# A's first head group in natural token order with 2 or 3 key blocks per query block, and factors per token spread by way of DRAM

## The chip, the cores and the metric

The kernel runs on one core of one Trainium2 chip. The metric is the device time of one execution in microseconds (us), the median of several. Engines: PE (TensorE; PEld is its weight load), DVE (VectorE), ACT (ScalarE), POOL (GpSimd) and SP (SyncE). In this kernel SP's queue issues the weight loads and POOL's queue issues transfers of intermediate data.

## The reference, cut to what matters

An encoder of two layers on 512 tokens of width 1024. Each layer projects the normalised input by one wide matrix and feeds three branches. Only the parts that the change touches stand here:

```python
DEPTH, SEQ, D_MODEL = 2, 512, 1024
A_GROUPS = ((128, 1), (512, 4), (2048, 16))   # (window, dilation), two heads of 64 each
def layer(x):
    xn = rms_norm(x, norm1_g)                  # one factor per token
    aq, ak, av, bq, bk, bv, cq, ck, cv, cg, gates = split(xn @ w_in)
    # A: each query attends to i + dilation*j, |j| <= window/(2*dilation), softmax;
    #    group outputs are weighted by their shares of the softmax denominators
    o, lse = dilated_window_attention(rope(norm(aq)), rope(norm(ak)), av, dilation, half)
    ya = o * softmax(lse over groups)          # one factor per token and head
    yb = rms_norm(diff_attention(...), b_out_norm_g) * c             # 4 heads of 128
    yc = silu(cg) * rms_norm(bidirectional_retention(...), c_out_norm_g)   # 4 heads of 128
    g = sigmoid(gates)
    x = x + (g0 * (ya @ w_br_a) + g1 * (yb @ w_br_b) + g2 * (yc @ w_br_c)) @ w_o
    x = x + square(relu(rms_norm(x, norm2_g) @ w_mlp1)) @ w_mlp2
```

A's first group has window 128 and dilation 1: a query sees the 64 tokens before and after it, so in natural order a block of 128 queries meets keys of its own block and of the neighbours at either side only.

## The kernel before, in words

All tensors are fp32. Each operand of a large product is split in two fp32r parts (`xh`, `xl`; `hi`, `lo`), and three products stand for one (`mm3`, `gemm`). Weights come in units of 512 KB at most by SP's queue into four raw buffers; `refine` has ACT make `whi` and DVE make `wlo` of each, two units ahead of PE, in three buffers each. `gemm` accumulates a chunk in four PSUM banks (`acc0` to `acc3`), which DVE or ACT evacuate while PE goes on with the next chunk.

Activations between the large products have the feature in the partition and the 512 tokens along the row. Token 4p+j stands in column 128j+p, so each of the four blocks of 128 columns holds every fourth token. In that order the window of A's first group (heads with g = 0) reaches into all four blocks: `a_dense_scores` (L650) scores a block of 128 queries against all 512 keys and adds a mask, and `dense_out` (L562) turns all 16 blocks of 128x128 over by PE transposes (`to_keys`, L535, tile ps_to_keys), splits them and multiplies them by V (tile ps_a_tail). The groups with dilation 4 and 16 need only blocks on the diagonal (`a_diag_scores`, `a_diag_out`).

A factor per token (the RMS factors of the two norms, the norm factor of each B or C head, the shares of A's groups) is computed on DVE with the token in the partition, as a tile of 128x4 or 128x24. To scale a tile that has the feature in the partition, the factor must stand along the row in all partitions. `norm_spread` (L423) broadcasts the factor along the row and transposes it on PE (tile ps_norm), and ACT copies it out as `rB`. `thread_a` (L709) copies A's shares to 128x512 (`wx`) and transposes them (ps_thread_a). `head_norm` (L579) transposes the head's output y to tokens in partitions (ps_yt), takes sums of squares, scales there by the factor (`yn`), transposes back (ps_yb), and then applies gain and gate.

Order: `build` makes one program of all operations. The main thread is the chain of gemms in the order of `sequence`; the side threads (prep, A, B, C, norm of a head) yield after each piece, with a lag in PE time (`W`). `emit` (L1064) then puts the program into one queue per engine: at each step the operation that can start first by the kernel's own reckoned durations, and among several the one that stands first in the program. A transfer by POOL counts 1.0 there, and 2.0 until its data can be used. Each engine then runs its queue in that order; an operation whose input is late holds up all that stands behind it on its engine.

POOL's queue before holds only 24 transfers: in each layer the eight residual tiles `xr` loaded ahead of the output projection, and between the layers the eight stores of `xspill`.

Of the kernel before, what the change touches and what calls it, by code (L numbers as in the profile page):

```python
# [9 lines left out]
FT = mybir.dt.float32  # L10
# [6 lines left out]
P = 128  # L17
# [10 lines left out]
C_ID, C_DL, C_U, C_M1, C_M2 = 0, 128, 1024, 1920, 2048  # L28
C_CP, C_SP, C_CC, C_SC, C_END = 2176, 2208, 2240, 2496, 2752
# [13 lines left out]
def shape_constants():  # L43
# [5 lines left out]
    blob[:, C_U:C_M1] = np.where(np.abs(dl) <= 64, 0.0, NEG).reshape(P, 896)  # L49
# [63 lines left out]
class Trunk:  # L113
# [202 lines left out]
    def setup(self):  # L316
# [31 lines left out]
        self.xspill = [a["x"], self.dp.tile([KD, P, SEQ], FT, name="xspill")]  # L348

# [121 lines left out]
    def prep(self, w, jp):  # L471
# [38 lines left out]
        own = [slice(64 * m, 64 * m + 64) for m in range(2)]  # L510
        for m in range(2):
            self.act(qk[own[m], m:4:2, qs], b[own[m]])
# [9 lines left out]
    def score(self, w, ms, j, pss, n=None):  # L522
        qk = w["qk"]
        js = slice(j * P, (j + 1) * P)
        ks = slice(0, SEQ) if n is None else js
# [36 lines left out]
    def dense_out(self, vt, ws, av):  # L562
        for jk in range(NJ):
            hi, lo = self.to_keys(ws, jk)
            yield ("wait", "av")
            if isinstance(vt, tuple):
                self.av_all(av, vt, jk, hi, lo, jk == 0, jk == NJ - 1)
            else:
                self.mm(av, vt[:, jk, :], hi, jk == 0, False)
                self.mm(av, vt[:, jk, :], lo, False, jk == NJ - 1)  # L570
            yield
# [7 lines left out]
    def head_norm(self, l, branch, h, y, s):  # L579
# [8 lines left out]
        for j in range(NJ):  # L588
            self.act(y[:, j * P:(j + 1) * P], b[:, j * P:(j + 1) * P], AF.Square, accum_out=ss[:, j:j + 1])
# [6 lines left out]
        else:  # L596
# [3 lines left out]
        yn = self.U(name="yn")  # L600
        self.tt(yn.rearrange("p (j e) -> p j e", j=NJ), b.rearrange("p (j e) -> p j e", j=NJ),
                g[:, :, None].to_broadcast([P, NJ, P]), OP.mult)
        yield ("wait", "yb")
        b2 = self.ps(name="ps_yb")
        for j in range(NJ):
            self.tr(b2[:, j * P:(j + 1) * P], yn[:, j * P:(j + 1) * P], self.ident)
        out = self.y[l, branch]
        if branch == 1:
            out[h] = self.split(b2, "yn", scale=gain)
        else:  # L610
            self.stt(yn, b2, gain, self.silu[l][h], OP.mult, OP.mult)
            self.silu[l][h] = None
            yield
            out[h] = self.split(yn, "yn")
# [34 lines left out]

    def a_dense_scores(self, w, m, st, nmx, den):  # L650
        for j in range(NJ):
            ps = self.ps(name="ps_a_dense_scores")
            self.score(w, (m,), j, (ps,))
            sm = self.U(name="sm")
            mx = self.tiny(1, "mx1")
            mask = self.blob[:, C_U - P + (3 - j) * P:C_U - P + (7 - j) * P]
# [52 lines left out]
    def thread_a(self, l):  # L709
# [5 lines left out]
        for g in range(3):  # L715
# [3 lines left out]
            n_, d_ = nmx[:, g * 8:g * 8 + 8], den[:, g * 8:g * 8 + 8]  # L719
            for m in range(2):  # L720
# [6 lines left out]
                tail = self.a_tail(l, w, m, g, st, ys)  # L727
        yield from tail
        nm = self.tiny(8, "amin", 2)
# [3 lines left out]
        for g in range(3):  # L733
# [485 lines left out]
```

## Time and profile before

| | |
|---|---|
| median of 3 runs | 1721.14 us (1721.01 to 1721.66) |
| profiled execution | 1721.42 us, span 1719.6 us (1.8 us lie outside the span) |
| granted TensorE clock, mean | 1.000 |
| PE busy | 1709.5 us (99%) |
| DVE busy | 1094.3 us (64%) |
| ACT busy | 813.0 us (47%) |
| POOL busy | 13.3 us (1%) |
| DMA | 93 GB/s over the span |

Matmuls of PE overlap, so the time that one takes of the engine is the distance between starts, not its own duration. "Idle before" names what an engine waited for. The layers are alike; the first one's attention part lies between 30 and 450 us, its MLP follows until 860 us, and the second layer repeats this.

### The profile page before, as it was taken

The page shows a single profiled execution, that of the slowest core. Times are in us where ns is not written, and L with a number is a line of the kernel's source. Part 1 is how long each engine was busy: PE and PEld are TensorE (multiplying, and loading weights), DVE is VectorE, ACT ScalarE, POOL GpSimd, SP SyncE. Part 2 cuts the span into 40 slices and gives each one's busy share as a digit, 9 for nine tenths or more (in the row PEclk, how much of TensorE's full clock was granted, in tenths as well). Part 3 has the DMA queues.
Part 4 walks back from the last instruction along what each step waited for, and adds up shares of the span by engine and source line. Part 5 has one row for each costly group of instructions (what it writes and reads, how often), then busy time and mean ns, then how long its engine had stood idle before and what let it go on. Part 6 is the DMA issues. An engine that isn't in the chain of part 4 may idle for free. (4 is left out here: it accounts for less than half of the span.)

```text
span 1719.6 us, 21537 instructions
## 1 busy us (share of the span) xinstructions
PE 1709.5 (99%) x8120; PEld 1454.8 (85%) x8120; DVE 1094.3 (64%) x2126; ACT 813.0 (47%) x1529; POOL 13.3 (1%) x29
## 2 busy tenths in 40 slices
PE   8999999999999999999999999999999999999999
PEld 8889988888888888888898899888888888888887
DVE  8788897887655343434468788888867543434342
ACT  7676674655344232323457666646543441414141
POOL 0000000000000000000000000000000000000000
PEclk9999999999999999999999999999999999999999
DMA  6212212223322222222332222222232222222221
GB/s 222 106 60 72 83 56 95 78 74 105 104 98 98 98 98 98 98 95 93 107 123 86 71 68 78 80 74 86 74 123 90 96 97 98 98 98 98 98 92 68
DMA packets 47960, 160.64 MB, mean 93 GB/s; under 512 B 5616, under 2 KB 6256, under 8 KB 47728
## 3 DMA queue, kind: packets, MB, share of 16 engines
q1 hardware_dynamic: 45072, 151.84, 26.0%
q0 software_dynamic: 1920, 6.29, 1.0%
q8 instruction: 64, 1.05, 0.2%
q10 hardware_dynamic: 864, 1.13, 0.2%
q14 instruction: 40, 0.33, 0.1%
HBM read 155.05 MB, written 4.19 MB: 93 GB/s over the span
## 5 line engine op out<-in xcount | busy, mean ns | idle before, releaser
L185 DVE TENSOR_TENSOR wlo<-raw,whi 128x1024 fp32r<-128x1024 f32 (+2 forms) x297 | 345.0, 1162 | 456.7 <-ACT whi L175 456.0
L175 ACT ACTIVATE whi<-raw 128x1024 fp32r<-128x1024 f32 (+2 forms) x297 | 300.2, 1011 | 629.8 <-PE acc L224 560.7
L224 PE MATMUL acc<-xgh,whi 128*128 128x512 f32 x960 | 377.1, 393 | 0.0
L224 PE MATMUL acc<-xgl,whi 128*128 128x512 f32 x960 | 374.7, 390 | 0.0
L224 PE MATMUL acc<-xgh,wlo 128*128 128x512 f32 x960 | 374.2, 390 | 0.0
L224 PEld LDWEIGHTS acc<-xgh,wlo 128*128 128x128 f32 x960 | 180.3, 188 | 37.6
L224 PEld LDWEIGHTS acc<-xgh,whi 128*128 128x128 f32 x960 | 180.3, 188 | 37.4 <-DVE gate L194 0.8
L224 PEld LDWEIGHTS acc<-xgl,whi 128*128 128x128 f32 x960 | 180.4, 188 | 36.1
L224 PE MATMUL acc<-whi,xgh 128*128 128x384 f32 (+1 forms) x576 | 202.5, 355 | 6.0 <-ACT whi L175 5.5
L224 PE MATMUL acc<-wlo,xgh 128*128 128x384 f32 (+1 forms) x576 | 201.7, 350 | 0.0
L224 PE MATMUL acc<-whi,xgl 128*128 128x384 f32 (+1 forms) x576 | 201.3, 349 | 0.0
L224 PE MATMUL acc<-hh,whi 128*128 128x512 f32 x512 | 199.2, 389 | 0.0
L224 PE MATMUL acc<-hl,whi 128*128 128x512 f32 x512 | 199.2, 389 | 0.0
L224 PE MATMUL acc<-hh,wlo 128*128 128x512 f32 x512 | 199.2, 389 | 0.0
L224 PEld LDWEIGHTS acc<-whi,xgh 128*128 128x128 f32 x576 | 108.8, 189 | 13.0 <-ACT whi L175 5.8
L224 PEld LDWEIGHTS acc<-wlo,xgh 128*128 128x128 f32 x576 | 109.2, 189 | 6.0 <-DVE wlo L185 0.3
L224 PEld LDWEIGHTS acc<-whi,xgl 128*128 128x128 f32 x576 | 109.0, 189 | 5.3
L224 PEld LDWEIGHTS acc<-hl,whi 128*128 128x128 f32 x512 | 96.1, 188 | 20.0
L224 PEld LDWEIGHTS acc<-hh,wlo 128*128 128x128 f32 x512 | 96.1, 188 | 19.9
L224 PEld LDWEIGHTS acc<-hh,whi 128*128 128x128 f32 x512 | 96.1, 188 | 19.9
L175 ACT ACTIVATE qk<-ps_prep 64x512 fp32r<-64x512 f32 (+1 forms) x144 | 69.8, 485 | 20.3 <-DVE qk L185 11.4
L185 DVE TENSOR_TENSOR xr<-xr,acc 128x512 f32<-128x512 f32 (+1 forms) x81 | 54.6, 678 | 30.6 <-PE acc L224 30.1
(199 smaller groups left out, 2225.3 us busy)
## 6 DMA issues: line engine op xcount, KB each, us to landing
raw<-in_weights_dram SPq DMA_DIRECT2D x236, 512.0 KB, 3.2
raw<-in_weights_dram SPq DMA_DIRECT2D x55, 384.0 KB, 3.0
xt<-in_x_dram SPq DMA_DIRECT2D x8, 256.0 KB, 5.1
xr<-in_x_dram POOLq DMA_DIRECT2D x8, 256.0 KB, 3.9
xspill<-xr POOLq DMA_DIRECT2D x8, 256.0 KB, 2.5
xr<-xspill POOLq DMA_DIRECT2D x8, 256.0 KB, 3.5
blob<-in_blob_dram SPq DMA_DIRECT2D x1, 1024.0 KB, 8.4
raw<-in_weights_dram SPq DMA_DIRECT2D x4, 256.0 KB, 2.6
```

The lines of the kernel that those rows point to most:

```text
L175: lambda: self.nc.scalar.activation(out, in_, func, **k))
L185: self.dve(out, [out], [a, b], lambda: self.nc.vector.tensor_tensor(out, a, b, op=op))
L224: self.op("PE", d, [out], [lhsT, rhs], lambda: self.nc.tensor.matmul(out, lhsT, rhs, start=start, stop=stop))
```

## The change

Three edits.

1. A's first group keeps queries, keys and values in natural token order. `keep_in_order` writes queries and keys into natural order while they are evacuated from PSUM; `reorder` stores V (two tiles of 256 KB) to DRAM and loads it back in four pieces each; a block of queries is scored against the 2 or 3 blocks next to it, with a mask table of three blocks; `band_out` transposes 10 blocks in three groups (4, 3 and 3) where 16 were transposed, and multiplies with 256 or 384 columns. The output goes back to the old token order as it is evacuated, and the statistics (8 minima, 8 denominators per partition) go back by way of DRAM (`reorder_stats`).
2. `norm_spread` becomes `spread`: the tile of factors is stored to DRAM as rows of 512, and a load that reads the same row for all partitions puts it along the row. The same serves A's shares (6 rows, 64 partitions each) and the norm factor of each B and C head, which is then applied to y itself, in the feature layout, so the transpose back goes.
3. The sum of squares writes its unused product to PSUM, so that y stays.

```diff
     def norm_spread(self, r):
-        b2 = self.ps(name="ps_norm")
-        for j in range(NJ):
-            self.tr(b2[:, j * P:(j + 1) * P], r[:, j:j + 1].to_broadcast([P, P]), self.ident)
-        rB = self.U(name="rB")
-        self.act(rB, b2)
-        return rB
+        return self.spread(r, 1, "rB")[0]
+
+    def spread(self, r, n, name, rows=P):
+
+        d = self.dp.tile([n, SEQ], FT, name=self.uid("row"))
+        self.dma(self.nc.gpsimd, d.rearrange("i (j p) -> p (i j)", j=NJ), r, 2)
+        out = []
+        for i in range(0, n, P // rows):
+            t = self.U(name=name)
+            for h in range(P // rows):
+                v = d[i + h]
+                self.dma(self.nc.gpsimd, t[rows * h:rows * h + rows], bass.AP(tensor=v.tensor, offset=v.offset, ap=[[0, rows], [1, SEQ]]), 256)
+            out.append(t)
+        return out
...
-        yn = self.U(name="yn")
-        self.tt(yn.rearrange("p (j e) -> p j e", j=NJ), b.rearrange("p (j e) -> p j e", j=NJ),
-                g[:, :, None].to_broadcast([P, NJ, P]), OP.mult)
+        rows, = self.spread(g, 1, "yr")
         yield ("wait", "yb")
-        b2 = self.ps(name="ps_yb")
-        for j in range(NJ):
-            self.tr(b2[:, j * P:(j + 1) * P], yn[:, j * P:(j + 1) * P], self.ident)
         out = self.y[l, branch]
         if branch == 1:
-            out[h] = self.split(b2, "yn", scale=gain)
+            self.stt(y, y, gain, rows, OP.mult, OP.mult)
         else:
-            self.stt(yn, b2, gain, self.silu[l][h], OP.mult, OP.mult)
+            self.tt(y, y, rows, OP.mult)
+            self.stt(y, y, gain, self.silu[l][h], OP.mult, OP.mult)
...
+    def reorder(self, l, w):
+
+        for h in range(2):
+            d = self.vspill[l][h]
+            self.dma(self.nc.gpsimd, d.rearrange("(p j) c -> p j c", j=NJ), w["v"][h], 256)
+            v = self.U((P, NJ, P), FR, "v")
+            for j in range(NJ):
+                self.dma(self.nc.gpsimd, v[32 * j:32 * j + 32],
+                         d.rearrange("(a i j) c -> j i a c", a=NJ, j=4)[j], 64)
+            w["v"][h] = v
...
+    def reorder_stats(self, l, st):
+        d = self.sspill[l]
+        for j in range(4):
+            self.dma(self.nc.gpsimd, d.rearrange("c (a i j) -> j i (c a)", a=NJ, j=4)[j], st[32 * j:32 * j + 32], 2)
+        o = self.tiny(16, "ast", 2)
+        self.dma(self.nc.gpsimd, o.rearrange("p (c j) -> p c j", j=4), d.rearrange("c (p j) -> p c j", j=4), 8)
+        return o
+
+    def band_out(self, v, e, av):
+        for group in ((0, 3), (1,), (2,)):
...
+            for jk, q0, q1, o in at:
+                n = (q1 - q0) * P
+                self.mm(av[:, q0 * P:q1 * P], v[:, jk, :], hi[:, o:o + n], jk == 0, False)
+                self.mm(av[:, q0 * P:q1 * P], v[:, jk, :], lo[:, o:o + n], False, jk == 2)
...
     def a_dense_scores(self, w, m, st, nmx, den):
         for j in range(NJ):
-            ps = self.ps(name="ps_a_dense_scores")
-            self.score(w, (m,), j, (ps,))
-            sm = self.U(name="sm")
+            k0, k1 = self.near(j)
+            n = (k1 - k0) * P
+            ps = self.ps((P, n), name="ps_a_dense_scores")
+            self.score(w, (m,), j, (ps,), slice(k0 * P, k1 * P))
+            sm = self.U((P, n), name="sm")
...
+        self.copy(nmx[:, 0:8], ast[:, 0:8])
+        self.copy(den[:, 0:8], ast[:, 8:16])
...
+        wx = self.spread(wt, 6, "wx", 64)
         yield
         for g in range(3):
-            wx = self.U((P, NJ, 2, 64), name="wx")
-            self.copy(wx, wt[:, g * 8:g * 8 + 8].rearrange("p (m j) -> p j m", j=NJ)[:, :, :, None].to_broadcast(
-                [P, NJ, 2, 64]))
             yield ("wait", "wx")
-            b = self.ps(name="ps_thread_a")
-            for j in range(NJ):
-                self.tr(b[:, j * P:(j + 1) * P], wx[:, j].rearrange("p m d -> p (m d)"), self.ident)
-            self.tt(ys[g], ys[g], b, OP.mult)
+            self.tt(ys[g], ys[g], wx[g], OP.mult)
```

What the engines hold: PE had 8120 matmuls in the trace; the change removes 128 transposes (64 of ps_yb, 24 of ps_thread_a, 24 of ps_to_keys, 16 of ps_norm) and cuts 64 matmuls of 512 columns to 256 (32 of them) or 384 (32). On DVE about as many instructions of 128x512 come as go; six copies `wx` go. POOL gets 84 transfers more.

The order on POOL's queue in the first layer. Before, the first transfers are the residual loads, late in the layer:

```order
L324 MEMSET warm 128x2
L234 DMA xr_1107<-in_x_dram 128x512
L234 DMA xr_1108<-in_x_dram 128x512
L234 DMA xr_1109<-in_x_dram 128x512
L234 DMA xr_1110<-in_x_dram 128x512
```

With the change, ahead of these, from the last load of V on (sspill and ast are the statistics of A's first group, awt A's shares, hg the norm factor of a head):

```order
L236 DMA v_257<-vspill_103 32x4x128
L236 DMA sspill_106<-ast_157_255 32x16x1 x4
L236 DMA ast_312<-sspill_106 128x4x4
L236 DMA row_452<-awt_451 128x24x1
L236 DMA wx_453<-row_452 64x512
L236 DMA wx_454<-row_452 64x512
L236 DMA wx_455<-row_452 64x512
```

The three loads of wx then come a second time, for the other 64 partitions, so wx_453 is whole with the fourth load.

The order on DVE where A's shares are applied (ya are A's outputs). Before, from the shares on, the copies that feed the transposes stand next to them, and the first product comes 17 rows after the shares:

```order
L185 TENSOR_TENSOR awt_447<-ad_444,az_354_446 128x24
L219 COPY wx_450<-awt_447 128x512
L219 COPY wx_464<-awt_447 128x512
...
L194 SCALAR_TENSOR_TENSOR vl_404<-acc_406,nr_85_173,vh_403 128x128
L185 TENSOR_TENSOR ya_278<-ya_278,ps_thread_a_451 128x512
L194 SCALAR_TENSOR_TENSOR vl_404<-acc_407,nr_85_173,vh_403 128x128
```

With the change, from the shares on (21 rows later the product, which needs wx_453):

```order
L187 TENSOR_TENSOR awt_451<-ad_448,az_352_450 128x24
L187 TENSOR_TENSOR yl_433<-yl_433,ps_a_tail_432 64x256
...
L187 TENSOR_TENSOR wlo_466<-raw_425,whi_465 128x768
L196 SCALAR_TENSOR_TENSOR vl_408<-acc_411,nr_85_179,vh_407 128x128
L187 TENSOR_TENSOR ya_287<-ya_287,wx_453 128x512
L187 TENSOR_TENSOR qk_234<-ps_prep_457,qk_234 64x2x256
L196 SCALAR_TENSOR_TENSOR vl_408<-acc_412,nr_85_179,vh_407 128x128
```

Behind the product stand an evacuation of query parts (qk) and the evacuation of the fourth PSUM bank of the chunk that has just ended (vl_408<-acc_412).

The order on DVE at the norm of B's third head. Before, from the last step of the factor hg on:

```order
L194 SCALAR_TENSOR_TENSOR hg_1018<-rt_929_1021,hg_1018 128x4
L185 TENSOR_TENSOR yn_1022<-ps_yt_1014,hg_1018 128x512
L185 TENSOR_TENSOR gate_1025<-acc_957,rB_216 128x512
L185 TENSOR_TENSOR wTl_1028<-ps_to_keys_1026,wTh_1027 128x512
L185 TENSOR_TENSOR wlo_1034<-raw_973,whi_1033 128x1024
L194 SCALAR_TENSOR_TENSOR ynl_1038<-ps_yb_1036,ghead,ynh_1037 128x512
```

With the change:

```order
L196 SCALAR_TENSOR_TENSOR hg_1021<-rt_926_1024,hg_1021 128x4
L187 TENSOR_TENSOR gate_1028<-acc_959,rB_222 128x512
L187 TENSOR_TENSOR wTl_1031<-ps_to_keys_1029,wTh_1030 128x512
L187 TENSOR_TENSOR wlo_1037<-raw_965,whi_1036 128x1024
L187 TENSOR_TENSOR wTl_1041<-ps_to_keys_1039,wTh_1040 128x512
L187 TENSOR_TENSOR wTl_1046<-ps_to_keys_1044,wTh_1045 128x512
L196 SCALAR_TENSOR_TENSOR y_1012<-y_1012,ghead,yr_1026 128x512
L187 TENSOR_TENSOR wlo_1048<-raw_987,whi_1047 128x1024
```

The product with the factor, which followed at once from PSUM, now stands five instructions later and needs yr, which two transfers of POOL bring; the split of a weight unit (wlo_1048) stands behind it.

## Rows read from the trace of the kernel before

**Rows 1.** Page, busy time of each engine, share of the span and instructions

```profile
PE 1709.5 (99%) x8120; PEld 1454.8 (85%) x8120; DVE 1094.3 (64%) x2126; ACT 813.0 (47%) x1529; POOL 13.3 (1%) x29
```

**Rows 2.** Waits: who waited for whom, us in total, times, longest

```profile
ACT whi L175 <- PE acc L224: 560.7, 173, 5.0
...
PE acc L224 <- ACT whi L175: 5.5, 1, 5.5
```

**Rows 3.** Windows: stretch and its length, then busy us (instructions) by engine

```profile
215.00:258.00 43.00, 42.70 (x201) 35.91 (x201) 40.99 (x90) 33.39 (x65) 0.00 (x0) 1.00 0.18 56
```

**Rows 4.** Chain that ended last: start, us, what

```profile
1210.77 0.91 PE ps_b_scores L224 x4
...
1235.60 0.44 PE ps_yb L228 x4
...
1383.73 0.44 PE ps_norm L228 x4
```

**Rows 5.** Timeline of PE, matmuls of 256 columns: start, us, engine, line, operation

```profile
99.31 0.64 PE L224 MATMUL ps_a_diag_scores<-qk 128*128 128x256 f32 x4
99.79 0.40 PE L224 MATMUL acc<-whi,xgl 128*128 128x512 f32 x1
```

**Rows 6.** Timeline of PE, first and thirteenth of a run of 384 columns

```profile
163.01 0.34 PE L224 MATMUL acc<-whi,xgl 128*128 128x384 f32 x1
...
165.10 0.33 PE L224 MATMUL acc<-whi,xgl 128*128 128x384 f32 x1
```

**Rows 7.** Page, DMA issues of POOL's queue: count, KB each, median us to landing

```profile
xr<-in_x_dram POOLq DMA_DIRECT2D x8, 256.0 KB, 3.9
xspill<-xr POOLq DMA_DIRECT2D x8, 256.0 KB, 2.5
xr<-xspill POOLq DMA_DIRECT2D x8, 256.0 KB, 3.5
```

**Rows 8.** Timeline of POOL, one issue of 128 rows of 2 KB

```profile
428.62 0.54 POOL L234 DMA_DIRECT2D xr<-in_x_dram  x1 [1.54 <-PE acc L224]
```

**Rows 9.** Page, DMA queues: packets, MB, share of 16 engines' span

```profile
q1 hardware_dynamic: 45072, 151.84, 26.0%
...
q10 hardware_dynamic: 864, 1.13, 0.2%
```

**Rows 10.** Timeline of DVE, A's first group: last V part, last score, first use

```profile
35.74 0.49 DVE L194 SCALAR_TENSOR_TENSOR v<-park,nr,v 128x64 fp32r<-128x64 f32 x2
...
93.07 0.15 DVE L189 TENSOR_SCALAR anm<-mx 128x1 f32<-128x1 f32 x1
...
149.92 0.16 DVE L185 TENSOR_TENSOR amin<-anm 128x8 f32<-128x8 f32 x1
```

**Rows 11.** Tile ps_a_tail: ns min/median/max, first and last start

```profile
L224 PE MATMUL ps_a_tail<-wTh,v x16: 389/394/500, 88.5 to 956.7; 128*128 128x512 f32 x16
```

**Rows 12.** Timeline of DVE, A's shares and the fourth bank's evacuation

```profile
154.64 0.18 DVE L185 TENSOR_TENSOR awt<-ad,az 128x24 f32<-128x24 f32 x1
...
165.98 0.35 DVE L194 SCALAR_TENSOR_TENSOR vl<-acc,nr,vh 128x128 fp32r<-128x128 f32 x1
```

**Rows 13.** Timeline of DVE, norm factors of B's third and fourth heads

```profile
422.29 0.16 DVE L194 SCALAR_TENSOR_TENSOR hg<-rt,hg 128x4 f32<-128x4 f32 x1
...
429.90 1.23 DVE L185 TENSOR_TENSOR wlo<-raw,whi 128x1024 fp32r<-128x1024 f32 x1 [2.30 <-ACT whi L175]
...
438.33 0.16 DVE L194 SCALAR_TENSOR_TENSOR hg<-rt,hg 128x4 f32<-128x4 f32 x1
...
446.34 0.69 DVE L185 TENSOR_TENSOR gate<-acc,rB 128x512 f32<-128x512 f32 x1 [0.62 <-PE acc L224]
```

**Rows 14.** Timeline of PE, B's projection begins

```profile
447.50 0.39 PE L224 MATMUL acc<-ynh,whi 128*128 128x512 f32 x1
```

**Rows 15.** Timeline of DVE, the second norm's factor and its first use

```profile
523.39 0.16 DVE L194 SCALAR_TENSOR_TENSOR nr<-rt,nr 128x4 f32<-128x4 f32 x1
...
531.81 0.68 DVE L194 SCALAR_TENSOR_TENSOR rl<-acc,rB 128x512 f32<-128x512 f32 x1
```

More of the change, by code (lines that the diff above doesn't have):

```diff
@@ L26 @@
 NEG = -1e30
[L28 to L29 removed]
+C_ID, C_DL, C_U, C_M1, C_M2 = 0, 128, 1024, 1408, 1536
+C_CP, C_SP, C_CC, C_SC, C_END = 1664, 1696, 1728, 1984, 2240
 N_U = 55
@@ L48, in shape_constants @@
     blob[:, C_DL:C_U] = dl.reshape(P, 896)
-    blob[:, C_U:C_M1] = np.where(np.abs(dl) <= 64, 0.0, NEG).reshape(P, 896)
+    tn = 4 * (p % 32) + p // 32
+    near = 128 * (np.arange(3)[None, :, None] - 1) + tn[None, None, :] - tn[:, None, None]
+    blob[:, C_U:C_M1] = np.where(np.abs(near) <= 64, 0.0, NEG).reshape(P, 384)
     dp = p[:, None] - p[None, :]
@@ L348, in setup @@
         self.xspill = [a["x"], self.dp.tile([KD, P, SEQ], FT, name="xspill")]
+        self.vspill = [[self.dp.tile([SEQ, P], FR, name=f"vspill{l}{h}") for h in range(2)] for l in range(DEPTH)]
+        self.sspill = [self.dp.tile([4, SEQ], FT, name=f"sspill{l}") for l in range(DEPTH)]
     def setup2(self):
@@ L510, in prep @@
         own = [slice(64 * m, 64 * m + 64) for m in range(2)]
+        if w["in_order"]:
+            yield from self.keep_in_order(w, jp, b, own)
+            return
         for m in range(2):
@@ L519, in prep, with score @@
         yield
-    def score(self, w, ms, j, pss, n=None):
+    def score(self, w, ms, j, pss, ks=slice(0, SEQ)):
         qk = w["qk"]
         js = slice(j * P, (j + 1) * P)
-        ks = slice(0, SEQ) if n is None else js
         for m, ps in zip(ms, pss):
@@ L648, in weave, with near, in_order @@
                     gens.remove(g)
+    @staticmethod
+    def near(a):
+        return max(0, a - 1), min(NJ, a + 2)
+    @staticmethod
+    def in_order(x):
+        return x.rearrange("p (j a i) -> p a j i", j=4, a=NJ)
+    def reorder(self, l, w):
[7 more added lines that the diff above has]
+            w["v"][h] = v
@@ new lines, in keep_in_order @@
+    def keep_in_order(self, w, jp, b, own):
+        qk = w["qk"]
+        to = lambda rows, x: qk[rows, x].rearrange("p (a j i) -> p j a i", a=NJ, j=4)[:, 2 * jp:2 * jp + 2]
+        ev = lambda rows, x: qk.bitcast(FT)[rows, x].rearrange("p (a j i) -> p j a i", a=NJ, j=4)[:, 2 * jp:2 * jp + 2]
+        fr = lambda rows, c: b[rows, c].rearrange("p (j a i) -> p j a i", j=2, a=NJ)
+        for m in range(2):
+            for c in range(2):
+                self.act(to(own[m], m + 2 * c), fr(own[m], c))
+        yield
+        for m in range(2):
+            for c in range(2):
+                self.tt(to(own[1 - m], m + 2 * c), fr(own[m], c), ev(own[m], m + 2 * c), OP.subtract)
+        for m in range(2):
+            self.act(to(own[1 - m], 4 + m), fr(own[m], 1))
+            self.act(to(own[m], 4 + m), ev(own[1 - m], 2 + m))
+        yield
@@ new lines, in reorder_stats @@
+    def reorder_stats(self, l, st):
[7 more added lines that the diff above has]
+        for group in ((0, 3), (1,), (2,)):
+            b = self.ps(name="ps_to_keys")
+            at, n = [], 0
+            for jk in group:
+                q0, q1 = self.near(jk)
+                at.append((jk, q0, q1, n))
+                for j in range(q0, q1):
+                    i = jk - self.near(j)[0]
+                    self.tr(b[:, n:n + P], e[j][:, i * P:(i + 1) * P], self.ident)
+                    n += P
+            hi, lo = self.U((P, n), FR, "wTh"), self.U((P, n), FR, "wTl")
+            self.act(hi, b[:, 0:n])
+            self.tt(lo, b[:, 0:n], hi.bitcast(FT), OP.subtract)
+            yield ("wait", "av")
+            for jk, q0, q1, o in at:
+                n = (q1 - q0) * P
+                self.mm(av[:, q0 * P:q1 * P], v[:, jk, :], hi[:, o:o + n], jk == 0, False)
+                self.mm(av[:, q0 * P:q1 * P], v[:, jk, :], lo[:, o:o + n], False, jk == 2)
+            yield
@@ L765, in a_tail @@
             av = self.ps(name="ps_a_tail")
-            yield from self.dense_out(w["v"][m], st, av)
+            yield from self.band_out(w["v"][m], st, av)
             t = self.U(name="yl")
             self.act(t[0:64], av[64:128])
-            self.tt(y[64 * m:64 * m + 64], t[0:64], av[0:64], OP.add)
+            block = lambda x: x.rearrange("p (a j i) -> p a j i", a=NJ, j=4)
+            self.tt(self.in_order(y[64 * m:64 * m + 64]), block(t[0:64]), block(av[0:64]), OP.add)
         else:
```

21 lines of the change are left out of this document (12 added, 9 removed).

## The prediction, made before the changed kernel ran

> **What bounds the kernel now.** I read the page's busy times first, then the waits, then the stretches of DVE, then the chain that ended last. PE is busy for 1709.5 of 1719.6 us, and no other engine passes 64% [rows 1]. A busy PE need not be a full one, so the waits decide: the largest that PE has is one of 5.5 us, at the start, while ACT waits 560.7 us in all for PE to free the buffers of split weights [rows 2]. Work of the other engines therefore stands ready before PE asks for it, and the split of weights runs as early as PE allows, two units ahead. The chain that ended last is nearly all PE. A microsecond of PE work taken out should come back as a microsecond, unless a new wait takes it. One stretch speaks for caution: between 215 and 258 us DVE is busy for 40.99 of 43 us, about as full as PE [rows 3].
>
> **What goes from PE.** The chain gives prices as distances between starts, with the change between kinds of work in them: four transposes take 0.44 us (0.11 each), four matmuls of 512 columns 0.91 us (0.2275 each) [rows 4]. Four matmuls of 256 columns take 99.79 - 99.31 = 0.48 us (0.12 each) [rows 5]. Twelve of 384 columns take 165.10 - 163.01 = 2.09 us (0.174 each) [rows 6].
>
> Transposes: 64 of ps_yb, 24 of ps_thread_a, 16 of ps_norm and 24 of ps_to_keys go, 128 x 0.11 = 14.1 us. A group of three is priced like part of a group of four; if each of the eight groups of three paid 0.05 us more for the change of work, that would be 0.4 us less.
>
> Matmuls of A's first group: 32 of scores and 32 of ps_a_tail, 512 columns each. Half of each now have 256 columns and half 384: 32 x (0.2275 - 0.12) + 32 x (0.2275 - 0.174) = 3.4 + 1.7 = 5.1 us. Together 19.2 us of PE time go, 9.6 in each layer. All of it lies where PE is without gaps, so I count all of it.
>
> On DVE and ACT about as much comes as goes. DVE loses six copies to wx and part of the masks, gains four small copies and eight more, shorter evacuations of queries. Nothing of it is on PE's path, since these engines wait for PE.
>
> **What comes: round trips through DRAM.** A factor now leaves DVE, is stored by POOL, waits for that store, is loaded by POOL into all partitions, and only then is used by DVE. The trace has no store of single values, so I bound it. A store of 256 KB lands in 2.5 us and a load of 256 KB in 3.5 to 3.9 us [rows 7]; POOL spends 0.54 us on issuing 128 rows of 2 KB [rows 8]. One packet costs a DMA engine 0.26 x 1719.6 x 16 / 45072 = 159 ns on the weight queue, where it has over 3 KB, and 0.002 x 1719.6 x 16 / 864 = 64 ns on the queue with the smallest [rows 9].
>
> For a norm factor, 512 values. Low end: the store takes as long as that of 256 KB, 2.5 + 3.5 = 6.0 us. High end: every value is a packet of its own, because the layout puts the four values of a partition 512 bytes apart in DRAM. Then issue 4 x 0.54 = 2.2, movement 512 / 16 x 64 ns = 2.0, and the rest of a store (2.5 less 128 / 16 x 159 ns = 1.2), 5.4 in all; with 0.54 + 3.9 for the load 9.8 us. A cost under zero is excluded, since PE and ACT do not get the transfer's work. I take 9, near the high end, as the layout is as the high end has it.
>
> For A's shares, 3072 values, and wx_453 whole with the fourth load of 64 partitions. Low end 2.5 + 4 x 0.27 + 3.5 = 7.1 us. High end: issue 24 x 0.54 = 13.0, movement 3072 / 16 x 64 ns = 12.3, rest 1.2, then 4 x 0.54 + 3.9 = 6.1, in all 32.6 us one after the other; 20.3 us where issue hides the movement. I take 15 us: between the low end and the overlapped high end, nearer the latter, again for the layout.
>
> What covers them, one by one:
>
> V's way to DRAM and back: V of A's first group is complete at 36.2 us [rows 10] and first used at 88.5 [rows 11], 52 us. Ten issues of 0.54, a store of 2.5 and a load of 3.9 make 11.8 us. Twice that would still be hidden. The statistics: the last score of that group is at 93.1 and the first use at 149.9 [rows 10], 57 us for five transfers of at most some 6 us each. POOL's queue works in order, so each wait there holds the transfers behind it; in this part of the layer nothing urgent stands behind.
>
> The second norm: the factor is ready at 523.55 and first used at 531.81 [rows 15]. The PSUM bank in question is needed again after three more banks, 18 x 0.2275 = 4.1 us later, so the use may start as late as 531.8 + 4.1 - 0.7 = 535.2, a cover of 11.7 us against 9. Hidden. The first norm's factor has several chunks of time.
>
> The heads' norms, 16 in all. The waiting instruction is a DVE product, and what stands behind it on DVE is what matters. At B's third head the factor is ready at 422.45; before the next split of weights at 429.90 DVE waits 2.30 us for ACT in any case [rows 13]. So a round trip of 6.8 us delays nothing, and one of 9 us delays that split by 2.2 us, which two units ahead (48 x 0.2275 = 10.9 us of PE work) absorb. At B's fourth head the factor is ready at 438.5 and the evacuation of the third bank, at 446.34, now stands behind the product [rows 13]. PE starts the next chunk at 447.50 [rows 14] and asks for that bank 12 x 0.2275 = 2.7 us later, at 450.2; product and evacuation take 0.69 each, so the product may start at 448.8. Cover 10.3 us against 9. Hidden, but with little to spare. C's heads have rows of the other heads' factors between, and their projection comes chunks later. I count nothing for the heads; without cover each microsecond past 10.3 would cost up to 2 us, one for B's fourth head in each layer.
>
> A's shares are the one that I do not see covered. They are ready at 154.8, and the evacuation of the fourth bank, at 165.98, now stands behind the product [rows 12], with half an evacuation of queries between. PE asks for that bank about 4.1 us later, at 170.1; 0.69 + 0.69 + 0.35 us of DVE work have to be done by then, so the product may start at 168.3, a cover of 13.5 us. With 15 us PE waits 1.5 us in each layer, 3 us in all.
>
> The sum: the profiled execution of before took 1721.4 us (span 1719.6, 1.8 around it). 1721.4 - 19.2 + 3.0 = 1705.2 us. The median of the runs lies 0.3 us below that execution, so 1705 us.
>
> **The rivals.** First, everything is hidden: the shares come in under 13.5 us, and 1721.4 - 19.2 = 1702 us stands, a little less where small waits of PE go too. For it: PE's waits are so few that the order leaves room everywhere. Against it: a transfer in which each of 3072 values goes by itself has no like in the trace.
>
> Second, single values are dear, and the kernel is slower. Place: the DVE product that waits for wx_453, once in each layer. Price: at the high end of 32.6 us PE waits 32.6 - 13.5 = 19.1 us each time, 38 us in all, and 1721.4 - 19.2 + 38.2 = 1740 us. It decides from 13.5 + 9.6 = 23.1 us on, where the wait eats what a layer gains. For it: the layout, and the issue price if it goes by packets. Against it: issue and movement one after the other is the worst case, and with overlap at 20.3 us the loss is 6.8 us a layer and the kernel still faster, at 1716 us. A rule of the Trainium skill stands on its side: the page "DMA: Bandwidth & Descriptors", in "Rules for kernel authors", says that a transfer whose last dimension is not contiguous becomes one descriptor per element. No run here shows that yet; by that rule the high ends would be the ones to take, 1740 us, and 1716 us with overlap.
>
> Third, DVE takes over as the bound in the attention part: PE asks earlier for work that DVE cannot give earlier, and half of the gain stays, 1721.4 - 9.6 = 1712 us. For it: 40.99 of 43 us [rows 3]. Against it: it is one stretch in each layer, none of the removed work lies in it, and over the whole span DVE has a third of its time free [rows 1].
>
> **How the numbers follow.** My forecast, 19.2 us gone and 0 to 7 us given back at A's shares (1702.5 to 1710), has a chance of 0.52. Everything hidden (below 1702.5) has 0.20. DVE as the bound, or shares near the overlapped high end (1710 to 1717.7), has 0.10. Two tenths of a percent, 3.4 us, is about what a measurement of this kernel can tell from no change; a result within that has 0.06. Slower, by dear values, has 0.12. So faster is 0.82, the same 0.06, slower 0.12. For 8 in 10 the range leaves out the far tail of the dear values and some of the lowest times: 1699 to 1720.
>
> **What would show it.** In the profile after, PE's busy time should be about 1690 us and PE should have 128 matmuls less. The waits should show DVE waiting for a transfer at ya<-ya,wx for some us and PE waiting for DVE (vl or qk) about 1.5 us right after; the products y<-y,yr should wait little, and PE not at all for them. The issue of row<-awt on POOL and its landing tell single values' price: over 23 us would prove me wrong on the sign, under 13 us on the 3 us given back. If PE's gaps instead follow the wTl, sd or nm of DVE in the stretch after 215 us, DVE was the bound. If four transposes or the shorter matmuls cost other distances than above, the 19.2 us is wrong.

## The result and the profile after

The changed kernel takes 1852.05 us (median of 4 runs, 1851.7 to 1855.42) against 1721.08 for the kernel before: a ratio of 1.0766 [1.0749, 1.0783]. I had forecast 1705 and a range that ended at 1720. It is slower by 131 us, and the forecast has the wrong sign.

The page's busy times of the changed kernel, to be held against [rows 1]:

```profile
PE 1719.3 (93%) x7992; PEld 1460.3 (79%) x7992; DVE 1086.7 (59%) x2128; ACT 810.4 (44%) x1529; POOL 66.2 (4%) x113
```

PE has the 128 instructions less that were forecast, and yet is busy 9.8 us longer. Its idle time is 1850.0 - 1719.3 = 130.7 us, where it was 10.1. So two things went wrong at once: PE stands still, and its work takes longer. The waits of PE (who waits for whom, us in total, times, longest) say for what it stands still; the kernel before had one wait of note [rows 2]:

```profile
PE acc L226 <- DVE gate L187: 44.4, 4, 17.9
PE acc L226 <- DVE vl L196: 38.5, 4, 11.8
PE acc L226 <- DVE gate L196: 16.0, 2, 8.0
PE ps_yt L230 <- ACT y L177: 11.8, 2, 6.3
PE acc L226 <- DVE rl L196: 8.9, 2, 4.5
```

These 119.6 us are 14 stops, seven in each layer. PE's timeline has those of the first layer (start and us of the matmul behind the stop, what it is, then the length of the stop and who ended it); two more, at 172.62 and 482.80 us, stand further down:

```profile
334.32 0.66 PE L226 MATMUL acc<-whi,xgh 128*128 128x384 f32 x1 [16.95 <-DVE gate L187]
371.83 0.80 PE L226 MATMUL acc<-ynh,whi 128*128 128x512 f32 x1 [8.03 <-DVE vl L196]
431.98 0.80 PE L226 MATMUL acc<-xgh,whi 128*128 128x512 f32 x1 [8.02 <-DVE gate L196]
...
505.44 0.80 PE L226 MATMUL acc<-ynh,whi 128*128 128x512 f32 x1 [4.58 <-DVE gate L187]
596.34 0.47 PE L226 MATMUL acc<-xgh,whi 128*128 128x512 f32 x1 [4.37 <-DVE rl L196]
```

The stop at 172.62 belongs to A's shares, 334.32 to C's heads, 371.83, 431.98, 482.80 and 505.44 to B's four heads, and 596.34 to the second norm. Over both layers the heads cost 88.4 us (C's 34.8, B's 16.1, 16.0, 11.9 and 9.6), the shares 22.4 and the second norm 8.9.

The instructions waited for (evacuations, V's low part, a copy) are cheap and old. The waits of DVE and ACT show what stands ahead of them in their queues:

```profile
DVE y L196 <- DMA yr<-row: 70.9, 8, 11.5
DVE y L187 <- DMA yr<-row: 35.1, 5, 11.1
...
DVE ya L187 <- DMA wx<-row: 22.0, 2, 11.6
```

```profile
ACT ynh L177 <- DVE y L196: 91.9, 12, 9.7
```

Every one is a product that waits for a row of factors to come back from DRAM, or the split behind it. Most of the stops need no more than DVE's own queue. So at B's second head:

```profile
427.75 0.75 DVE L196 SCALAR_TENSOR_TENSOR y<-y,ghead,yr 128x512 f32<-128x512 f32 x1 [8.54 <-DMA yr<-row]
...
431.24 0.69 DVE L196 SCALAR_TENSOR_TENSOR gate<-gate,acc 128x512 f32<-128x512 f32 x1
```

Behind the product that waits stands `gate`, which empties the PSUM bank that PE needs next, and PE goes on at 431.98. The DMA issues (count, KB each, median us from issue to landing) name the slow part of the trip:

```profile
yr<-row POOLq DMA_DIRECT2D x16, 256.0 KB, 4.7
...
row<-hg POOLq DMA_DIRECT2D x16, 2.0 KB, 9.2
row<-nr POOLq DMA_DIRECT2D x4, 2.0 KB, 9.9
row<-awt POOLq DMA_DIRECT2D x2, 12.0 KB, 14.8
```

A load of 256 KB takes 4.7 us, where [rows 7] had 3.5 and 3.9. The store of 2 KB takes 9.2 us, almost four times that of 256 KB in [rows 7].

One kind of stop goes by way of a second engine. Here it is in full, at B's third head, which [rows 13] shows before. POOL's timeline (start, us, instruction, idle before it):

```profile
466.48 0.76 POOL L236 DMA_DIRECT2D row<-hg  x1 [43.10 <-DVE hg L196]
476.71 0.54 POOL L236 DMA_DIRECT2D yr<-row  x1 [9.46 <-PE ps_b_tail L226]
```

DVE at the same place:

```profile
466.03 0.16 DVE L196 SCALAR_TENSOR_TENSOR hg<-rt,hg 128x4 f32<-128x4 f32 x1
...
480.85 0.75 DVE L196 SCALAR_TENSOR_TENSOR y<-y,ghead,yr 128x512 f32<-128x512 f32 x1 [10.67 <-DMA yr<-row]
```

ACT:

```profile
481.63 0.63 ACT L177 ACTIVATE ynh<-y 128x512 fp32r<-128x512 f32 x1 [8.92 <-DVE y L196]
482.17 0.58 ACT L177 ACTIVATE y<-ps_b_tail 128x512 f32<-128x512 f32 x1
```

And PE:

```profile
482.80 1.12 PE L230 MATMUL ps_yt<-eye,y 128*128 128x128 f32 x4 [5.52 <-ACT y L177]
...
484.14 0.63 PE L226 MATMUL acc<-xgl,whi 128*128 128x512 f32 x1
484.57 0.63 PE L226 MATMUL acc<-xgh,wlo 128*128 128x512 f32 x1
```

The factor is ready at 466.19 and used at 480.85: a trip of 14.7 us. ACT's queue has the high part of that head, `ynh`, next; it waits for the product. Behind it, in order, stands the copy of the next head's output, `y<-ps_b_tail`, whose matrix products were done at about 476; and PE's queue has the transposes of that copy (`ps_yt`) ahead of all further weight products. So PE stops for 5.52 us over a tile that nothing but the order of two queues held back.

What follows the stop is the second loss. Matmuls of 512 columns now start 0.43 us apart (484.57 - 484.14), against 0.23 in [rows 4]; from 488 us on it is 0.23 again. The windows of the changed kernel (stretch, length, busy us of PE, PEld, DVE, ACT, POOL, then the granted clock, DMA share, GB/s) show why:

```profile
483.00:487.00 4.00, 4.00 (x12) 3.32 (x12) 1.57 (x10) 2.38 (x9) 0.00 (x0) 0.50 0.77 258
```

Behind the stop the granted clock is 0.50 for some 4 us of work, that is 1.2 GHz, before PE has 2.4 GHz again. Where nothing waits, between 640 and 900 us, the granted clock is 1.00 throughout.

### The profile page after: what moved, and what is told of

Its sections match the earlier page's. It is cut to its first block, busy times and chain, and to the rows that moved or that the text cites. A ratio compares the mean times of both kernels' runs of the same rounds, so it can differ in the third digit from the quotient of the medians.

```text
span 1850.0 us, 21458 instructions
## 1 busy us (share of the span) xinstructions
PE 1719.3 (93%) x7992; PEld 1460.3 (79%) x7992; DVE 1086.7 (59%) x2128; ACT 810.4 (44%) x1529; POOL 66.2 (4%) x113
## 5 line engine op out<-in xcount | busy, mean ns | idle before, releaser
L226 PE MATMUL acc<-xgh,whi 128*128 128x512 f32 x960 | 383.0, 399 | 24.9 <-DVE gate L196 16.0
L226 PE MATMUL acc<-xgl,whi 128*128 128x512 f32 x960 | 378.6, 394 | 0.0
L226 PE MATMUL acc<-xgh,wlo 128*128 128x512 f32 x960 | 378.0, 394 | 0.0
L226 PE MATMUL acc<-whi,xgh 128*128 128x384 f32 (+1 forms) x576 | 205.8, 360 | 63.7 <-DVE gate L187 34.8
L226 PE MATMUL acc<-ynh,whi 128*128 128x512 f32 x176 | 73.0, 415 | 25.7 <-DVE vl L196 16.1
L177 ACT ACTIVATE qk<-ps_prep 64x256 fp32r<-64x256 f32 (+1 forms) x152 | 70.5, 468 | 27.0 <-DVE qk L187 14.9
```

What stands on the lines that cost most here:

```text
L177: lambda: self.nc.scalar.activation(out, in_, func, **k))
L226: self.op("PE", d, [out], [lhsT, rhs], lambda: self.nc.tensor.matmul(out, lhsT, rhs, start=start, stop=stop))
```

## The experiments

All ratios are against the kernel before, run on the same chip.

**Which edit.** Edit 1 alone (the norms, heads and shares spread by PE as before), and edit 2 alone, with edit 3, which it needs (A's first group as before).

```diff
 # edit 1 alone, against the changed kernel
-        return self.spread(r, 1, "rB")[0]
+        b2 = self.ps(name="ps_norm")
+        for j in range(NJ):
+            self.tr(b2[:, j * P:(j + 1) * P], r[:, j:j + 1].to_broadcast([P, P]), self.ident)
...
-        wx = self.spread(wt, 6, "wx", 64)
...
```

> Edit 1 alone: the first head group in natural order, with V and the statistics going through DRAM, while all factors are spread by PE transposes as before. Theory (the round trips of the spread factors are the whole loss): 24 transposes less (2.6 us) and shorter matmuls (5.1 us), no new wait on PE, so 1721 - 7.7 = 1713 us, clock 1.00. Rival (V's and the statistics' trips through POOL's queue hold PE up as well): above 1730 us, with PE or DVE waiting for v or ast.

Measured 1713.68 us (1712.83 to 1713.88), 0.9958 [0.9943, 0.9973]: 7.1 us gone.

> Edit 2 alone: all factors by way of DRAM, the first head group against all keys as before. Theory: 104 transposes less (11.4 us), all the waits of the changed kernel, some 140 us of idle time and slow clock, so 1721 - 11 + 140 to 150 = 1850 to 1860 us. Rival (the loss belongs in part to edit 1): under 1800 us.

Measured 1863.49 us (1858.77 to 1867.23), 1.0837 [1.0819, 1.0855]. Edit 1 gives what it was priced at (5.1 us of matmuls and 24 transposes, 7.7 us; PE is busy 1709.5 - 1701.7 = 7.8 us less). The whole loss, 143 us, is edit 2's.

**What makes the store slow.** The kernel before with eight extra stores in each layer's MLP, for which nothing waits, in different shapes: 512 values at neighbouring addresses as in the changed kernel (`adjacent`), the same in runs of 16 bytes (`runs`), each value 64 or 512 bytes from the next (`apart`, `faraway`), 512 values from 32 partitions whose values lie 16 bytes from one partition to the next (`few`), 128 values at neighbouring addresses (`quarter`), and 3072 values in either way (`sixrows`, `sixruns`).

```diff
+            self.dma(q, d.rearrange("i (j p) -> p (i j)", j=NJ), r, 2)          # adjacent
+            self.dma(q, d.rearrange("i (p j) -> p (i j)", j=NJ), r, 2)          # runs
+            self.dma(q, d.rearrange("(j p) k -> p j k", j=NJ)[:, :, 0], r, 2)   # apart: k of 16
...
```

> The kernel before with eight extra stores of small tiles in each MLP, one per chunk of the first product, which nothing waits for. Each has 512 values from 128 partitions but where said: adjacent (as the spread stores them, partition p next to partition p+1), runs (16 bytes of a partition together), apart (each value 64 bytes from the next), faraway (512 bytes), few (32 partitions of 16 values, 16 bytes apart, as the statistics), quarter (128 values, adjacent), sixrows (3072 values, adjacent, as the shares), sixruns (3072 values in runs of 16 bytes). Landing times. Theory 1 (partitions that write next to each other in DRAM get in each other's way): adjacent 9 us, apart and faraway 3 to 4, runs about 4. Theory 2 (each value costs the same): adjacent, apart and faraway all 9, quarter 4, runs 4, few 9. The time stays within 0.2% of before.

Measured once, 1721.15 us for the whole. The DMA issues:

```profile
adjacent<-pr POOLq DMA_DIRECT2D x2, 2.0 KB, 9.5
runs<-pr POOLq DMA_DIRECT2D x2, 2.0 KB, 1.9
apart<-pr POOLq DMA_DIRECT2D x2, 2.0 KB, 2.2
...
quarter<-pr POOLq DMA_DIRECT2D x2, 0.5 KB, 8.1
sixrows<-pr POOLq DMA_DIRECT2D x2, 12.0 KB, 16.0
sixruns<-pr POOLq DMA_DIRECT2D x2, 12.0 KB, 3.2
```

512 separate values 64 bytes apart land in 2.2 us (`faraway` and `few` as well), and 128 neighbours need 8.1. The price is not that of the number of values. It is paid where partitions write 4 bytes each right beside one another in DRAM; four neighbours from one partition in one piece cost nothing extra.

Such a store also holds up what else is on its way. The weight loads issued in the 13 us from the first `adjacent` store on:

```profile
raw<-in_weights_dram SPq DMA_DIRECT2D x2, 512.0 KB, 8.4
```

In the kernel before, the same two loads take 3.1 us (median). Beside the other `adjacent` and the `quarter` stores such loads take 7.2 to 8.0 us, beside `sixrows` 11.2 and 11.7, and beside `runs`, `apart`, `faraway` and `few` 3.1 to 3.3.

**The order alone.** The changed kernel with one thing different: the scheduler reckons what the transfers really take.

```diff
-            far = 2.0 if i in self.moves else BEHIND[e]
+            far = self.far.get(i, 2.0) if i in self.moves else BEHIND[e]   # 9.5 store, 15 six rows, 5 load
```

> The changed kernel with one thing different: where the order of the queues is made, the spread's transfers count with the durations that the changed kernel's trace showed (a store of factors 10.5 us, of the shares 16 us, a load 6 us, in place of 3 us each). The transfers are the same. Theory (the loss is the order, which puts the products where they would be ready after 6 us, and they then hold up DVE and ACT for the rest of 15 us): most waits go, PE's idle falls from 131 us to under 30, 1702 to 1725 us. Rival (the trips lie on the path whatever the order, since heads and shares are needed soon): above 1770 us.

Measured 1747.28 us (1742.88 to 1749.48), 1.0151 [1.0136, 1.0166]: about 105 of the 131 us come back by order alone, but not all, which missed the expectation. The longest waits of PE that are left:

```profile
PE acc L226 <- DVE gate L187: 15.1, 2, 7.6
PE acc L226 <- DVE rl L196: 8.8, 2, 4.5
```

With 7.1 us for `ynh` these are three stops in each layer, in the first one at 314 us (C's heads, one trip behind another), 461 us (B's projection waits for B's last head) and 547 us (the second norm): as I read it, the trip there is longer than what the order has to put before it.

**The store alone.** The changed kernel with the row kept in pieces of 16 bytes, so that the loaded row has another order and the products read it with a stride of four. Instructions and their order are unchanged.

```diff
-        self.dma(self.nc.gpsimd, d.rearrange("i (j p) -> p (i j)", j=NJ), r, 2)
+        self.dma(self.nc.gpsimd, d.rearrange("i (p j) -> p i j", j=NJ), r.rearrange("p (i j) -> p i j", j=NJ), 2)
...
-            self.tt(y, y, rows, OP.mult)
+            self.tt(self.cols(y), self.cols(y), self.jp(rows), OP.mult)   # jp: rows.rearrange("q (p j) -> q j p")
```

> The changed kernel with one thing altered: the row in DRAM keeps the four values of a partition next to each other (16 bytes in one piece) and the DVE products read the loaded row with a stride of four. Instructions, transfers and their order stay. Theory 1 (the loss comes from the store of 4-byte values of different partitions at neighbouring addresses): the store of one row lands in about 1.9 us in place of 9.2 and that of six rows in about 3.2 in place of 14.8, a head's trip falls from 14.7 to some 7.5 us and lies under the cover that the prediction gave it, and the time falls by more than 110 us to 1702 to 1715. Theory 2 (the order has no room for any trip, however short; the loads of 4.7 us and the queues behind them are enough): the waits shrink in proportion, about half of the loss stays, 1770 to 1800. Theory 3 (reads with a stride make DVE slower by more than the trips give): DVE products above 1.2 us and the time above 1740.

Measured 1715.93 us (1713.36 to 1718.31), 0.9971 [0.996, 0.9983], one microsecond above the range of the first theory. Page, then DMA issues:

```profile
PE 1690.4 (99%) x7992; PEld 1437.5 (84%) x7992; DVE 1135.8 (66%) x2128; ACT 812.3 (47%) x1529; POOL 60.6 (4%) x113
```

```profile
row<-hg POOLq DMA_DIRECT2D x16, 2.0 KB, 1.8
...
row<-awt POOLq DMA_DIRECT2D x2, 12.0 KB, 3.8
```

One layout in DRAM is worth 136 us. The same 7992 PE instructions now take 1690.4 us, 19.1 less than before the change and 28.9 less than in the changed kernel: with the stops the half clock is gone too. DVE is busy 49 us longer; that is the stride (below). The slow store in a better order gave back 105 us, the short store in the old order 136. So the loss comes from the two together: the scheduler reckons 6 us for a store and a load (1.0 and 2.0 for each), and the head's trip above takes 14.7.

**Store and order together.** As that run, and the scheduler reckons 2.5 us for a row's store, 4 for six rows and 5 for a load.

> As the run before, and the scheduler now reckons 2.5 us for the store of a row, 4 us for six rows and 5 us for a load, in place of 2 for each. If the remaining waits come from the order: 1700 to 1706 us and PE's idle time near that of the kernel before (10 us). If they come from real dependencies (B's last head ahead of its projection, the second norm ahead of the next bank): within 3 us of the run before.

Measured 1709.95 us (1709.59 to 1710.36), 0.9936 [0.9921, 0.9951]: 6 us come back, so neither expectation is met. PE's idle time is 15.4 us; of its waits 5.1 us are for `gate` and `wTl` of DVE. One of the products with a row, here and in the changed kernel (busy us, mean ns):

```profile
L196 DVE SCALAR_TENSOR_TENSOR rl<-acc,rB 128x512 f32<-128x512 f32 x64 | 66.9, 1066 | 0.1
```

```profile
L196 DVE SCALAR_TENSOR_TENSOR rl<-acc,rB 128x512 f32<-128x512 f32 x64 | 43.6, 684 | 14.2 <-DMA rB<-row 13.8
```

**Is it the norms' trip or the stride?** Three runs. First the norms' factors by PE's transposes again, all products still with the stride. (Here the order of the norms' factors along the row is left out of account: they stand in plain order and are read with the stride; instructions and shapes are as with the order kept.)

> As the run before, but the factors of the two norms of each layer are spread by four transposes of TensorE again (16 in all, 1.8 us of PE work more); heads and shares stay on the way through DRAM. If the second norm's trip holds up PE, this is 3 to 8 us faster than the run before; if it is covered, as the prediction had it (11.7 us of cover), 1 to 2 us slower.

Measured 1713.69 us (1713.23 to 1714.2), 0.9957 [0.994, 0.9974]: 3.7 us slower, so the norms' trip was not what held PE up. (The 16 transposes are priced at 1.8 us of it; the rest has no explanation here.) Then the norms' rows by way of DRAM, turned into plain order once by ACT, and the 120 products with them without a stride:

```diff
-        return self.spread(r, 1, "rB")[0]
+        t = self.spread(r, 1, "rp")[0]
+        rB = self.U(name="rB")
+        self.act(self.cols(rB), self.jp(t))
+        return rB
...
-                    self.tt(self.cols(z), self.cols(b), self.jp(self.rB), OP.mult)
+                    self.tt(z, b, self.rB, OP.mult)
```

> As the run with 16-byte runs and reckoned transfers (1709.95 us), but the factor row of the two norms of each layer is turned into plain order once, by ACT, and the 120 products with it read it without a stride (0.68 in place of 1.07 us each, 46 us of DVE). If the 5 us of PE's waits for gate and wTl that were left there come from DVE's slower reads: they go, and the time is 1701 to 1706 us, the removed 19.2 us in full. If they come from the trips: 1708 to 1711.

Measured 1705.42 us (1704.99 to 1706.29), 0.991 [0.9893, 0.9926]: faster than both kernels, 15.5 us below the one before. PE's busy time:

```profile
PE 1690.8 (99%) x7992; PEld 1437.8 (84%) x7992; DVE 1093.8 (64%) x2128; ACT 814.8 (48%) x1533; POOL 60.4 (4%) x113
```

Of PE's waits the 5.5 us at the start are left, which the kernel before has too [rows 2]; the next largest comes to 1.2 us in all, and PE no longer waits behind A's shares.

Last, that kernel with the norms' factors by PE's transposes (16 more):

> As the run before, with the two norms' factors of each layer spread by 16 transposes of TensorE (1.8 us) in place of the way through DRAM; only heads and shares go through DRAM. If the norms' trips are covered, as the prediction had it: 1 to 3 us slower than the run before. If the second norm's trip holds up PE: faster.

Measured 1707.5 us (1707.2 to 1707.67), 0.9921 [0.9906, 0.9936]: 2.1 us slower, about the 1.8 us that the transposes cost. With short stores the norms' trips are covered.

**Which queue turns a trip into a stop.** The kernel before with one head alone changed, B's third, in each layer; its factor goes by neighbouring values as in the changed kernel.

```diff
-        self.side.append([self.head_norm(l, branch, h, y, s), None])
+        self.side.append([(self.head_norm_row if (branch, h) == (1, 2) else self.head_norm)(l, branch, h, y, s), None])
```

> The kernel before with one head alone changed: the norm factor of B's third head, once in each layer, goes through DRAM as in the changed kernel (values at neighbouring addresses). The prediction's reading (only what stands behind the product on DVE matters; a trip of up to 14 us is absorbed by the split of weights two units ahead): 1720 to 1722. Rival (ACT waits for the product too, so the copy of the next head's y stands still behind it, PE's transposes of it wait 5 us, and the matmuls behind them run at half clock for some 4 us): two stalls of 5.5 us and 2 us each of clock, less 0.9 us of transposes, about 1735.

Measured 1741.56 us (1740.18 to 1743.43), 1.012 [1.0105, 1.0136]: 20.6 us for two trips. ACT's timeline in the first layer, then PE's wait, then a window right behind the stop:

```profile
441.38 0.63 ACT L175 ACTIVATE ynh<-y 128x512 fp32r<-128x512 f32 x1 [11.43 <-DVE y L194]
```

```profile
PE ps_yt L228 <- ACT y L175: 17.5, 2, 10.1
```

```profile
443.00:447.00 4.00, 4.00 (x13) 3.23 (x12) 1.84 (x13) 1.14 (x8) 0.00 (x0) 0.50 0.53 177
```

It is the stop seen in the changed kernel, alone. PE is busy 1713.6 us, 4.1 more than before with 8 transposes (0.9 us) less: the two stops cost 17.5 us of waiting and some 5.0 us of half clock. Then the same kernel with the high part `ynh` copied by DVE, so that nothing on ACT stands behind the product:

```diff
-        out[h] = self.split(y, "yn")
+        hi, lo = self.U(dt=FR, name="ynh"), self.U(dt=FR, name="ynl")
+        self.copy(hi, y)
+        self.tt(lo, y, hi.bitcast(FT), OP.subtract)
+        out[h] = hi, lo
```

> As the kernel with one head through DRAM (1741.6 us; trips of 18.3 and 15.6 us; PE waits 10.1 and 7.5 us for ACT's copy of the next head), with one instruction on another engine: the high part of that head, ynh, is copied by DVE and not by ACT, so that nothing on ACT stands behind the product. If ACT's queue is what made the trip cost time, and DVE's delay alone is absorbed by the split of weights two units ahead (10.9 us), as the prediction reckoned: PE waits under 3 us in all and 1719 to 1726 us. If DVE's queue stops PE just as well (the split wlo comes 11 us late): 1735 us or more.

Measured 1735.72 us (1734.98 to 1737.52), 1.0087 [1.0072, 1.0102]. PE's waits:

```profile
PE ps_yb L228 <- DVE yn L185: 10.7, 2, 5.7
```

and DVE in the first layer:

```profile
438.64 0.75 DVE L194 SCALAR_TENSOR_TENSOR y<-y,ghead,yr 128x512 f32<-128x512 f32 x1 [13.40 <-DMA yr<-row]
...
444.00 0.69 DVE L185 TENSOR_TENSOR yn<-ps_yt,hg 128x512 f32<-128x512 f32 x1
```

With ACT free, `ps_yt` runs on time, and PE stops one step later: the next head's whole norm (from `hf` to `yn`) stands on DVE behind the product and the split of weights, and its transposes `ps_yb` stand in PE's order. Some seven tenths of the loss stay (14.8 of 20.6 us). At this head ACT's queue is the first to bite, DVE's the second; neither alone is the cause. At B's other heads and at C's, PE's waits in the changed kernel name DVE from the start.

## Why the prediction was wrong

- **PE work removed, 19.2 us: right.** With the stops gone, PE is busy 19.1 us less (1709.5 to 1690.4) and 18.7 less in the fastest version. In the changed kernel the sum was hidden: 1719.3 - 1690.4 = 28.9 us of the same work at the lower clock. The difference of 130.4 us in span is -19.1 + 28.9 + 120.6 of idle time.
- **The price of a row's store: wrong, and outside its bounds.** I bounded it at 5.4 us by one packet for each value. It lands in 9.2 to 9.9 us, and the head's trip takes 14.7 where I took 9 and allowed 9.8. Nor is issuing what I priced: POOL takes 0.76 us for the 512 values of a head and 1.43 for the 3072 of the shares, where I had 2.2 and 13.0; the time lies behind the issue. Nor does the trace have a packet for each value: the pages count 2496 packets on POOL's queue with the extra stores and 1920 in the kernel before, 576 more for 17664 values. The row of the trace that I priced by (64 ns for a packet) says nothing on neighbouring writes. The form of the price was wrong: by values, 512 that lie apart would cost as much, and they land in 2.2 us. The rule of the Trainium skill that I weighed (page "DMA: Bandwidth & Descriptors", "Rules for kernel authors": one descriptor per element) does not tell these apart either, since both layouts have a last dimension that is not contiguous; no run here shows descriptors.
- **"I count nothing for the heads": wrong, and the step that cost most, 88.4 of 119.6 us.** I had worked out a cover for two of a layer's eight heads only. "What stands behind it on DVE is what matters" holds where PE waits for an evacuation behind the product: at B's fourth head the trip of 16.1 us (487.90 to 504.04) exceeds the cover of 10.3 by 5.8, and PE stops 4.6 and 5.0. But the same kind of stop comes at B's first two heads and at C's, for which I had no cover, 66.9 us in all. At B's third head the sentence is wrong. I gave it 6.8 us and 10.9 more by the weights two units ahead, which would have covered even 14.7. But ACT's `ynh`, and behind it the next head's copy, were not on my list, nor the next head's norm behind the split on DVE. The runs with one head show both: 17.5 us of waiting by the one queue, 10.7 by the other.
- **"C's heads have rows of the other heads' factors between": wrong.** POOL's queue holds a load behind the store that it waits for, and the next head's store behind both. POOL's timeline of the changed kernel:

```profile
294.91 0.80 POOL L236 DMA_DIRECT2D row<-hg  x1 [125.83 <-DVE hg L196]
304.56 0.55 POOL L236 DMA_DIRECT2D yr<-row  x1 [8.84 <-PE ps_b_scores L226]
305.10 1.51 POOL L236 DMA_DIRECT2D row<-hg  x2
315.38 1.10 POOL L236 DMA_DIRECT2D yr<-row  x2 [8.77 <-DMA row<-hg]
```

  Four trips take from 295 to 331 us one after another, and the longest stop of the layer, 16.95 us for `gate`, ends them at 334.3.
- **A's shares: the place right, the size not.** DVE and PE there, in the changed kernel:

```profile
150.56 0.18 DVE L187 TENSOR_TENSOR awt<-ad,az 128x24 f32<-128x24 f32 x1
...
170.69 0.69 DVE L187 TENSOR_TENSOR ya<-ya,wx 128x512 f32<-128x512 f32 x1 [10.41 <-DMA wx<-row]
```

```profile
172.62 0.66 PE L226 MATMUL acc<-whi,xgh 128*128 128x384 f32 x1 [10.60 <-DVE vl L196]
```

  The trip takes 20.0 us where I took 15, and PE stops 10.6 us, not 1.5, before the very bank that I named. The difference, 9.4 us, is what was covered, where I had 13.5. That is the rival "single values are dear" at its place, but at 20 us, below the 23.1 from which I let it decide; with a cover of 9.4 it decides from 19.0 on. The two stops there, 22.4 us, outweigh the 19.1 us of work saved by themselves. The heads, which that rival did not have, make the loss as large as it is.
- **The second norm: the reasoning right, the price not.** The factor is ready at 580.3 and first used here ([rows 15] shows before):

```profile
595.50 1.29 DVE L196 SCALAR_TENSOR_TENSOR rl<-acc,rB 128x512 f32<-128x512 f32 x2 [6.84 <-DMA rB<-row]
```

  15.2 us against a cover of 11.7 leaves 3.5, and PE stops 4.4.
- **V, the statistics: right.** Edit 1 alone has no new wait. **DVE as the bound: no.** No version shows it as the bound: 42 us less of DVE's work gave 4.5 us (1709.95 to 1705.42).
- **The clock: not considered.** I costed a stop at its length. It costs some 2 us more, long or short: 28.9 us for 14 stops of 4.4 to 17.9 us in the changed kernel, 12.9 for six (1703.3 us of PE against 1690.4) with the order reckoned, 5.0 for two with one head.

What I forecast is not what this kernel does, but it is what its idea does: with stores of 16 bytes, transfers reckoned as they are, and the norms' rows turned once, the time is 1705.42 us. That it meets the forecast to half a microsecond is in part luck: the 3 us that I gave back for A's shares are not waited for there.

## What to carry to other kernels

A transfer that takes the place of engine work puts a wait into in-order queues: list what stands behind the waiting instruction on every engine that touches its result, and the transfer queue too, down to the next instruction in PE's order, before calling it covered. Measure an unknown small transfer in a probe for which nothing waits, in two or three layouts, before building on it. If a scheduler orders the queues by reckoned durations, a wrong duration there can cost a great deal (some 105 us here).

## What the hardware showed that I had not expected

- A store of 512 values of 4 bytes lands in 9.5 us when different partitions' values are neighbours in DRAM, in 2.2 us when they are 64 bytes apart, and in 1.9 us when each partition writes 16 bytes in one piece; 128 neighbours take 8.1 us. With 32 partitions 16 bytes apart it is 2.2 us too. Why this is so, and from which distance on it is cheap for 128 partitions, was not tried.
- While such a store was under way, weight loads of 512 KB took 7.2 to 8.4 us in place of 3.1.
- After a stop of 5.5 us the granted clock was 0.50 for some 4 us of work, that is 1.2 of 2.4 GHz, and 512-column matmuls started 0.43 us apart.
- A DVE product of 512 columns takes 0.684 us, and 1.066 us with one operand read at a stride of four values (16 bytes): 0.75 ns more for each column. The Trainium skill points the same way. Its page "Vector Engine (DVE) Microarchitecture Reference", in "5.2 Measured stream behaviour on trn2 (trn3 not measured)", has a port at full rate only where elements come in runs of two or more adjacent words, and some 0.65 cycles more for each element that hops from region to region. It has no row for this stride. An estimate from its rows for one source that hops 4 KiB on every element, (1.73 - 1.054) ns x 512, is 0.35 us, against the 0.38 measured here.
